# Two-layer retention, S5 and GLA encoder on one core: S5 parameters in two parts, S5 gates between the S5 output pairs, and another product order in the GLU

## The chip, the cores and the metric

The kernel runs on one core of a Trainium2 chip. The metric is the device time of one execution in microseconds; the kernel before has a median of 1593.84 us over three runs (1593.65 to 1594.63). The engines are TensorE (PE in the rows, with its weight loads as PEld), VectorE (DVE), ScalarE (ACT), GpSimd (POOL) and SyncE (SP), whose queue issues the DMAs.

## The reference

The input is 512 positions of 1024 features in float32, and there are two layers (`DEPTH = 2`). Each layer is

```
h = RMSNorm(x);  z = h @ w_in
A: retention, 4 heads, rotary q and k, fixed decay per head, head norm, swish gate
B: S5, 16 groups x 16 channels, complex diagonal state of 64, both directions, GELU, GLU projection
C: gated linear attention (GLA), 4 heads, gate from a low-rank projection, both directions, swish gate
merged = sum over the branches of sigmoid(h @ w_m + b) * (branch projection)
x += merged @ w_out
x += (relu(RMSNorm(x) @ w_up) ** 2) @ w_down
```

and a last RMSNorm follows. The GLU of branch B is `(y @ W1) * sigmoid(y @ W2)`. The S5 parameters of both layers (the discretised decays `exp(lambda * dt)`, their powers and the input factors) are worked out from 96 columns of a constant block: an exponential of `log_dt`, an exponential of `Re(lambda) * dt`, and a sine and cosine of `Im(lambda) * dt`, each as a polynomial on tiles of 128 x 32.

## The kernel before

Features lie on the partitions and the 512 positions on the free axis. The weights come as 128 chunks of 128 x 1024 a layer. `weights()` (L95) handles one: a DMA on SP's queue brings `raw` (three buffers, 512 KB), ScalarE casts it to `whi` (L108), and VectorE subtracts to make the remainder `wlo` (L109); five buffers hold such pairs. Activations are split the same way (`split()`, L112: `mh`, `ml`). `col_tile()` (L116) then issues three matmuls of 512 columns for each k: high times high, high times low, low times high. With 1024 inputs that is 24 matmuls for a column tile.

One layer runs in this order: the projections for S5 (`u`), GLA and retention; GLA; retention; the swish gates (`silu()`, L354); the sigmoid gates of the merge (`gate()`, L361, with numbers 16 to 23 for branch C, 0 to 7 for A and 8 to 15 for B), each group followed by its branch's projection; the GLU outputs of branch B in four pairs (`for j2`, L396); `w_out` (L412); then the feed-forward part.

What sets the order of instructions on each engine is the tile framework's scheduler, which goes by the order in which the code is written, by priorities (`hp(...)`) and by anchors (`issue_after`, which keeps an instruction behind another one). S5's own work is a generator, `self.bg`. `bg_steps(n, ...)` (L1023) pulls `n` of its pieces, anchored behind the evictions of the column tile just issued, so that they lie among the projections; in layer 0 the pieces also prepare the S5 matrices (60 pieces), in layer 1 that was done during layer 0's feed-forward part (24 pieces). `for _ in self.bg` (L393) pulls whatever is left.

`s5_params()` runs once, on GpSimd, with two casts and shifts and one reciprocal on VectorE. Its tiles are called `sp`; VectorE's part of an exponential is L818 (CAST) and L820 (shift). In the retention, a tile `za` of q or k gets its rotary form from three steps: GpSimd multiplies the swapped copy `rsw` (brought by DMA) by the sine (L634), VectorE multiplies `za` by the cosine (L635) and adds the two (L636); `qfb` (L666) is a decayed copy of q, also on GpSimd, also behind a DMA.

One GLU output goes through ScalarE (sigmoid of the second product, L404), GpSimd (times the gate, L405), VectorE (times the first product `ps1`, L406, and plus the sum of the other branches, L407), ScalarE (`mh`, L113) and VectorE (`ml`, L114).

Of the kernel before, what the change touches and what calls it, by code (L numbers as in the profile page):

```python
# [17 lines left out]
P = 128  # L18
# [21 lines left out]
class Hybrid:  # L40
# [147 lines left out]
    def run(self):  # L188
        nc, io = self.nc, self.io
        self.cst = self.one([P, 2432], "cst")  # L190
        xp = [self.sb.tile([P, 2, 512], F32, tag="xp", bufs=4, name=self.nm("xp")) for _ in range(KT // 2)]
        self.x = [xp[j // 2][:, j % 2, :] for j in range(KT)]
        self.chunk = 0
        self.pre = {}
        with self.hp(25000):
            nc.sync.dma_start(self.cst[:, C_SM:C_N], io["cst"][:, C_SM:])
            nc.sync.dma_start(self.x[0], io["xT"][:, 0, :])
            self.prefetch(0, 0, 2)
            nc.sync.dma_start(self.x[1], io["xT"][:, 1, :])
            nc.sync.dma_start(xp[1], io["xT"][:, 2:4, :])  # L200
            self.prefetch(0, 1, 2)
            for j in (2, 3):
                nc.sync.dma_start(xp[j], io["xT"][:, 2 * j:2 * j + 2, :])
            nc.sync.dma_start(self.cst[:, 0:C_MB], io["cst"][:, 0:C_MB])
        nc.sync.dma_start(self.cst[:, C_MB:C_SM], io["cst"][:, C_MB:C_SM])
        self.xsrc = [io["xT"][:, j, :] for j in range(KT)]
        self.sm = self.cst[:, C_SM:C_N]
        self.ident = self.cst[:, C_ID:C_ID + P]
        self.ones = self.cst[:, C_ONE:C_ONE + P]

        zero, warm = self.slot(s="warm"), self.ms()
        with self.hp(40000):
            nc.vector.memset(zero, 0.0)
            for _ in range(3):
                nc.tensor.matmul(warm, zero[:, 0:P], zero, start=True, stop=True)
        self.warm = lambda: nc.tensor.matmul(warm, zero[:, 0:P], zero, start=True, stop=True)
        accs, h = [], []
        with self.hp(35000):
            for j in range(KT):
                h.append(self.scaled_split(self.x[j], self.sm[:, SM_G1 + j:SM_G1 + j + 1]))  # L220
        with self.hp(30000):
            for j in range(KT):
                self.acc_sq(accs, self.x[j], j, nc.vector)
        for l in range(self.depth):
            self.chunk = 0
            h, accs = self.layer(l, h, accs)
# [78 lines left out]
    def layer(self, l, h, acc):  # L305
        nc, io = self.nc, self.io
# [18 lines left out]
        cv = [self.v_tiles(l, h, r) for _ in range(2)]  # L325
        if l == 0:
            with self.tc.issue_after(gl[-1][1].ins), self.tc.issue_after(self.gq.ins):
                self.s5_params()
        gla_o = []
        with self.hp(8000):  # L330
            pend = []
# [21 lines left out]

        def silu():  # L354
            sw = self.silu_tile(l, h, R)
            self.bg_steps(2, self.ev, self.mmi, self.aev)
            return sw

        yc = [self.gla_out(l, hd, gla_o[hd], silu()) for hd in range(4)]
# [1 line left out]
        def gate(j):  # L361
            w = self.weights(l)
            ps = self.col_tile(w, h)
            with self.hp(15000):
                g = self.gslot()
                ev = nc.vector.tensor_mul(g, ps, R)  # L366
                act = nc.scalar.activation(g, g, AF.Sigmoid, bias=self.smc(l, SM_BM, j))  # L367
            self.bg_steps(n, ev, self.mmi, act)
            return g
# [3 lines left out]
        for j2 in range(4):  # L373
            w = self.weights(l)
            for i in range(2):
                j = 2 * j2 + i
# [6 lines left out]
        for j4 in range(2):  # L383
            w = self.weights(l)
            for i in range(4):
                j = 4 * j4 + i
# [2 lines left out]
                    nc.vector.tensor_mul(ga[j], ga[j], ps)  # L389
                    nc.gpsimd.tensor_add(m[j], m[j], ga[j])  # L390
        ms = []
        gb = [gate(8 + j) for j in range(8)]
        for _ in self.bg:  # L393
            pass
        yb = self.ysplit(yb)
        for j2 in range(4):  # L396
            w = self.weights(l)
            for i in range(2):
                j = 2 * j2 + i
                ps1 = self.col_tile(w, yb, base=i * 512)  # L400
                ps2 = self.col_tile(w, yb, base=i * 512 + 256)
                with self.hp(15000):
                    s = self.gslot(s="glu")
                    nc.scalar.activation(s, ps2, AF.Sigmoid)  # L404
                    nc.gpsimd.tensor_mul(s, s, gb[j])  # L405
                    nc.vector.tensor_mul(s, s, ps1)  # L406
                    nc.vector.tensor_add(s, s, m[j])  # L407
                    hi, lo = self.slot(F32R, s="mh"), self.slot(F32R, s="ml")
                    self.split(hi, lo, s)
                    ms.append((hi, lo))  # L410
# [345 lines left out]
    def s5_params(self):  # L756
        nc = self.nc
# [4 lines left out]
        def T(dt=F32, keep=None):  # L762
            if keep:
                self.kn += 1
                return self.spk[:, (self.kn - 1) * N:self.kn * N]
            if self.tn % 16 == 0:
                self.spt = self.slot(shape=(P, 16, N), s="sp")
            o = self.spt[:, self.tn % 16, :]
            self.tn += 1
            return o if dt == F32 else o.bitcast(dt)  # L770
# [11 lines left out]
        def ts(a, s1, op0, s2=None, op1=None):  # L782
            o = T()
            if s2 is None:
                e.tensor_scalar(o, a, s1, None, op0)
            else:
                e.tensor_scalar(o, a, s1, s2, op0, op1)
            return o

        def poly(f, cs):  # L790
            q = ts(f, cs[-1], ALU.mult)
            for c in cs[-2::-1]:
                e.tensor_scalar(q, q, c, None, ALU.add)  # L793
                e.tensor_tensor(q, q, f, ALU.mult)
            return q
# [8 lines left out]
        def stt(a, s, b, op0, op1):  # L804
            o = T()
            e.tensor_scalar(o, a, s, None, op0)
            e.tensor_tensor(o, o, b, op1)
            return o
# [32 lines left out]
        s = poly(f2, [-1.0 / 6, 1.0 / 120, -1.0 / 5040, 1.0 / 362880])  # L841
        s = stt(s, 1.0, ph, ALU.add, ALU.mult)
        cm = poly(f2, [-0.5, 1.0 / 24, -1.0 / 720, 1.0 / 40320, -1.0 / 3628800])
        for _ in range(2):
            s2 = stt(cm, 1.0, s, ALU.add, ALU.mult)
            cm = stt(s, -2.0, s, ALU.mult, ALU.mult)
            s = ts(s2, 2.0, ALU.mult)
        c = ts(cm, 1.0, ALU.add)
        nr = stt(E, 1.0, cm, ALU.mult, ALU.mult)
        nr = tt(nr, em, ALU.add)  # L850
        ni = mul(E, s)
# [263 lines left out]
def _layout(v, depth=2):  # L1115
# [11 lines left out]
    def blk(w, c0, n=P):  # L1127
        k = w.shape[0] // P
        return w[:, c0:c0 + n].reshape(k, P, n).transpose(1, 0, 2).reshape(P, k * n)
# [5 lines left out]
    for l in range(depth):  # L1135
        w, wm = A("w_in")[l], A("w_merge_gate")[l]
        ba, bb, bc = A("w_branch_a")[l], A("w_branch_b")[l], A("w_branch_c")[l]
        wo, f1, f2 = A("w_out")[l], A("w_ff1")[l], A("w_ff2")[l]
        ch = [blk(w, c) for c in (1024, 1152)]
# [8 lines left out]
        ch += [np.concatenate([blk(bc, P * (2 * i + j)) for j in range(2)], 1) for i in range(4)]  # L1148
        ch += [blk(wm, P * i) for i in range(8)]
        ch += [np.concatenate([blk(ba, P * (4 * i + j)) for j in range(4)], 1) for i in range(2)]  # L1150
        ch += [blk(wm, 1024 + P * i) for i in range(8)]
        for i in range(4):
            ch += [np.concatenate([blk(bb, P * (2 * i + j) + o) for j in range(2) for o in (0, D)], 1)]
        ch += [blk(wo, P * i) for i in range(8)]
        for q in range(4):
# [6 lines left out]
        gw, gb = A("gla_w_gate")[l], A("gla_b_gate")[l]  # L1162
# [25 lines left out]
    i = np.arange(P)  # L1188
# [38 lines left out]
```

## Time and profile before

| | |
|---|---|
| median of three runs | 1593.84 us |
| the profiled execution | 1593.98 us, of which the span of the instructions is 1592.2 us |
| TensorE busy | 1561.0 us (98%), 7862 matmuls |
| VectorE busy | 942.7 us (59%) |
| ScalarE busy | 583.9 us (37%) |
| GpSimd busy | 220.1 us (14%) |
| mean granted clock of TensorE | 0.992 |

TensorE's busy time also counts the stretches in which it runs at half clock and those in which matmuls start further apart than 0.225 us, so 98% busy does not mean that only 2% can be had. A better measure of a stretch is how many matmuls it issued against how many would have fitted at the steady distance. The profiled execution lies 0.14 us above the median, and 1.8 us of it are outside the span.

### The profile page before, as it was taken

Reading aid. Unit: us, or ns where it says so; the run is one execution under the profiler, and the core shown is the slowest. Engines: PE = TensorE matmul, PEld = TensorE weight load, DVE = VectorE, ACT = ScalarE, POOL = GpSimd, SP = SyncE. Lnnn points to the kernel's source line nnn. Section 1 sums busy time; section 2 is a strip of 40 time slices with the busy share of each in tenths; the row PEclk is TensorE's granted clock in tenths of the full one; section 3 lists DMA queues with packets and bytes.
Section 4 is the critical chain, followed back from the end, with each engine's and each line's share of the span. In section 5 each row is a group of like instructions: output and inputs, shape, how many; then the busy total and the mean of one; then the engine's idle time right before and its main releaser. Section 6 shows DMA issues by size and latency. Waiting matters only on the chain.

```text
span 1592.2 us, 20246 instructions
## 1 busy us (share of the span) xinstructions
PE 1561.0 (98%) x7862; PEld 1306.5 (82%) x7862; DVE 942.7 (59%) x1579; ACT 583.9 (37%) x909; POOL 220.1 (14%) x351
## 2 busy tenths in 40 slices
PE   9998999999899999999999999999999999999997
PEld 6878888888788888888889888888868888888897
DVE  6776899854655747434658859844356534343353
ACT  5432444343434343423435332432334423232242
POOL 0185211121220000000101211203022000000001
PEclk9999999999999999999999999999999999999999
DMA  6513224233332323232434322342233232323221
GB/s 211 167 42 111 76 83 125 80 123 109 113 99 68 116 69 122 81 105 93 154 116 142 106 80 67 89 139 92 98 106 126 93 99 90 103 93 106 93 67 54
DMA packets 60512, 163.35 MB, mean 103 GB/s; under 512 B 10556, under 2 KB 17212, under 8 KB 60416
## 3 DMA queue, kind: packets, MB, share of 16 engines
q1 hardware_dynamic: 60096, 161.01, 31.6%
q8 instruction: 62, 1.02, 0.3%
q0 software_dynamic: 320, 1.05, 0.3%
q14 instruction: 34, 0.28, 0.1%
HBM read 147.11 MB, written 6.52 MB: 96 GB/s over the span
## 4 chain that ended last, share of the span: by engine, by line
PE 84%; DVE 7%; POOL 4%; ACT 2%; issue 2%; DMA 1%; SPq 0%; DVEq 0%; POOLq 0%; ACTq 0%
PE mm L126 25%; PE mm L127 25%; PE mm L125 25%; POOL glu L405 1%; PE mm L286 1%; PE mm L284 1%; PE mm L282 1%; DVE wlo L109 1%; PE ms L1091 1%; DMA dup<-zc 1%; POOL sp L793 1%; DVE glu L406 1%; DVE glu L407 1%; PE ms L1051 1%; PE ms L707 0%
## 5 line engine op out<-in xcount | busy, mean ns | idle before, releaser
L127 PE MATMUL mm<-hh,wlo 128*128 128x512 f32 x1136 | 445.8, 393 | 0.8 <-DVE wlo L109 0.8
L125 PE MATMUL mm<-hh,whi 128*128 128x512 f32 x1136 | 446.0, 393 | 0.0
L126 PE MATMUL mm<-hl,whi 128*128 128x512 f32 x1136 | 445.7, 392 | 0.0
L108 ACT CAST whi<-raw 128x1024 fp32r<-128x1024 f32 (+1 forms) x258 | 265.9, 1040 | 266.3 <-PE mm L127 137.5
L109 DVE TENSOR_TENSOR wlo<-raw,whi 128x1024 fp32r<-128x1024 f32 (+1 forms) x258 | 334.2, 1297 | 34.2 <-PE mm L126 28.1
L127 PEld LDWEIGHTS mm<-hh,wlo 128*128 128x128 f32 x1136 | 213.9, 188 | 44.9 <-DVE wlo L109 1.2
L125 PEld LDWEIGHTS mm<-hh,whi 128*128 128x128 f32 x1136 | 213.9, 188 | 44.7 <-issue 1.0
L126 PEld LDWEIGHTS mm<-hl,whi 128*128 128x128 f32 x1136 | 213.7, 188 | 44.0 <-issue 0.7
L126 PE MATMUL mm<-fl,whi 128*128 128x512 f32 (+1 forms) x576 | 210.8, 366 | 0.0
L127 PE MATMUL mm<-fh,wlo 128*128 128x512 f32 (+1 forms) x576 | 210.3, 366 | 0.0
L125 PE MATMUL mm<-fh,whi 128*128 128x512 f32 (+1 forms) x576 | 209.6, 366 | 0.0
L125 PEld LDWEIGHTS mm<-fh,whi 128*128 128x128 f32 x576 | 108.6, 189 | 17.8
L126 PEld LDWEIGHTS mm<-fl,whi 128*128 128x128 f32 x576 | 108.6, 189 | 17.6
L127 PEld LDWEIGHTS mm<-fh,wlo 128*128 128x128 f32 x576 | 108.6, 189 | 17.6 <-DVE wlo L109 0.2
L178 POOL TENSOR_TENSOR acc<-acc,sq 128x512 f32<-128x512 f32 (+1 forms) x30 | 35.3, 1176 | 552.9 <-ACT sq L177 552.9
L463 DVE TENSOR_TENSOR x<-x,mm 128x512 f32<-128x512 f32 x56 | 38.4, 685 | 121.8 <-PE mm L127 121.8
L438 ACT ACTIVATE ht<-ht 128x512 f32<-128x512 f32 x64 | 40.5, 632 | 175.1 <-DVE ht L437 175.1
L437 DVE SCALAR_TENSOR_TENSOR ht<-mm,R 128x512 f32<-128x512 f32 x64 | 44.1, 689 | 94.6 <-PE mm L127 83.4
L367 ACT ACTIVATE g<-g,cst 128x512 f32<-128x512 f32 x48 | 34.8, 725 | 148.1 <-DVE g L366 148.1
L114 DVE TENSOR_TENSOR fl<-ht,fh 128x512 fp32r<-128x512 f32 x64 | 44.3, 692 | 70.4 <-ACT fh L113 70.2
L366 DVE TENSOR_TENSOR g<-mm,R 128x512 f32<-128x512 f32 x48 | 32.9, 685 | 86.1 <-PE mm L127 82.6
L125 PE MATMUL mm<-y,whi 128*128 128x512 f32 x160 | 62.6, 391 | 0.7 <-DVE glu L406 0.7
(267 smaller groups left out, 2068.4 us busy)
## 6 DMA issues: line engine op xcount, KB each, us to landing
raw<-wst SPq DMA_DIRECT2D x254, 512.0 KB, 3.7
dup<-zc SPq DMA_DIRECT2D x32, 128.0 KB, 3.3
rsw<-za SPq DMA_DIRECT2D x32, 64.0 KB, 2.0
qfb<-za SPq DMA_DIRECT2D x16, 128.0 KB, 2.7
x<-xT SPq DMA_DIRECT2D x8, 256.0 KB, 3.9
xs<-x SPq DMA_DIRECT2D x8, 256.0 KB, 2.8
x<-xs SPq DMA_DIRECT2D x8, 256.0 KB, 4.2
outT<-out SPq DMA_DIRECT2D x8, 256.0 KB, 2.7
```

What stands on the lines that cost most here:

```text
L108: nc.scalar.copy(hi[:, s], raw[:, s])
L109: nc.vector.tensor_sub(lo[:, s], raw[:, s], hi[:, s].bitcast(F32))
L114: self.nc.vector.tensor_sub(lo, src, hi.bitcast(F32))
L125: nc.tensor.matmul(ps, hi[:, o:o + P], a, start=first and k == 0, stop=False)
L126: nc.tensor.matmul(ps, hi[:, o:o + P], b, start=False, stop=False)
L127: self.mmi = nc.tensor.matmul(ps, lo[:, o:o + P], a, start=False, stop=last and k == n - 1)
L178: return (eng or (nc.vector if j == KT - 1 else nc.gpsimd)).tensor_add(accs[0], accs[0], t)
L366: ev = nc.vector.tensor_mul(g, ps, R)
L367: act = nc.scalar.activation(g, g, AF.Sigmoid, bias=self.smc(l, SM_BM, j))
L437: ev = nc.vector.scalar_tensor_tensor(t, ps, 0.0, R2, ALU.max, ALU.mult)
L438: act = nc.scalar.square(t, t)
L463: ev = nc.vector.tensor_add(self.x[j], self.x[j], ps)
```

## The change

There are four edits.

1. `s5_params()` is made a generator with one `yield`. Its first part, up to the sine and cosine, is issued before the loop over the layers, where the start's own work is; the second part stays behind the GLA gates with the same anchors as before.
2. `silu()` pulls three S5 pieces, not two.
3. The eight gates of branch B (`gb`) are no longer all issued ahead of the S5 outputs: two are issued, then the rest of S5 is drained, and two more precede each further pair of GLU outputs. The weight chunks are laid out in this order too.
4. In the GLU, VectorE multiplies the gate by `ps1` (not the sigmoid's result by `ps1`), which can run beside the sigmoid; GpSimd then multiplies the sigmoid's result by that product, and VectorE adds the other branches.

```diff
+        self.params = self.s5_params()
+        next(self.params)
         for l in range(self.depth):
...
             with self.tc.issue_after(gl[-1][1].ins), self.tc.issue_after(self.gq.ins):
-                self.s5_params()
+                next(self.params, None)
...
-            self.bg_steps(2, self.ev, self.mmi, self.aev)
+            self.bg_steps(3, self.ev, self.mmi, self.aev)
...
-        gb = [gate(8 + j) for j in range(8)]
+        gb = [gate(8 + j) for j in range(2)]
         for _ in self.bg:
             pass
         yb = self.ysplit(yb)
         for j2 in range(4):
+            if j2:
+                gb += [gate(8 + 2 * j2 + i) for i in range(2)]
             w = self.weights(l)
...
                     nc.scalar.activation(s, ps2, AF.Sigmoid)
+                    nc.vector.tensor_mul(gb[j], gb[j], ps1)
                     nc.gpsimd.tensor_mul(s, s, gb[j])
-                    nc.vector.tensor_mul(s, s, ps1)
                     nc.vector.tensor_add(s, s, m[j])
...
         c = ts(cm, 1.0, ALU.add)
+        yield
         nr = stt(E, 1.0, cm, ALU.mult, ALU.mult)
...
-        ch += [blk(wm, 1024 + P * i) for i in range(8)]
         for i in range(4):
+            ch += [blk(wm, 1024 + P * (2 * i + j)) for j in range(2)]
             ch += [np.concatenate([blk(bb, P * (2 * i + j) + o) for j in range(2) for o in (0, D)], 1)]
```

The changed file has up to five lines more, so L634 of before is L638 after, L666 is L670, L818 and L820 are L822 and L824, L366 is L368, L404 is L408, and the GLU's three products and sums (L405, L406, L407) are L410, L409 and L411.

**GpSimd in layer 0's retention.** These are consecutive instructions of GpSimd before, around the second sine product of the retention (`rsw_1269`); `sp`, `pwt` and `cst` belong to the S5 parameters.

```order
L776 TENSOR_TENSOR cst<-sp_884 128x32
L887 TENSOR_TENSOR pwt_909<-cst 128x32
L888 TENSOR_TENSOR pwt_910<-cst 128x32
L634 TENSOR_TENSOR rsw_1269<-rsw_1269,sin_1192 128x512
L887 TENSOR_TENSOR pwt_909<-cst 128x32
L888 TENSOR_TENSOR pwt_910<-cst 128x32
```

And this is where the first sine products stand after.

```order
L895 TENSOR_TENSOR cst<-pwt_909,pwt_910 128x32x2
L894 TENSOR_TENSOR cst<-pwt_909,pwt_910 128x32x2
L638 TENSOR_TENSOR rsw_1228<-rsw_1228,sin_1192 128x512
L670 TENSOR_TENSOR qfb_1489<-qfb_1489,cst 128x512
L638 TENSOR_TENSOR rsw_1269<-rsw_1269,sin_1192 128x512
L670 TENSOR_TENSOR qfb_1496<-qfb_1496,cst 128x512
```

The parameters now end ahead of the first sine product, and the `qfb` product of the first `za` has come between the first and the second sine product. The first part of the parameters stands at the very start of GpSimd's list.

**VectorE at the start.** These are VectorE's instructions before, from the gate matrix `wg` to the statistics `nv` of the first norm.

```order
L486 TENSOR_TENSOR wlrs_268<-wlr_266,wlrs_268 128x8x16
L509 SCALAR_TENSOR_TENSOR wg_290<-wgh_301,cst,wgr_297 98x512
L109 TENSOR_TENSOR wlo_307<-raw_304,whi_306 128x1024
L109 TENSOR_TENSOR wlo_346<-raw_343,whi_345 128x1024
L158 TENSOR_SCALAR nv_151<-ms_142 128x4
```

And after:

```order
L490 TENSOR_TENSOR wlrs_371<-wlr_369,wlrs_371 128x8x16
L513 SCALAR_TENSOR_TENSOR wg_393<-wgh_404,cst,wgr_400 98x512
L822 CAST sp_179<-sp_179 128x32
L824 TENSOR_SCALAR sp_179<-sp_179 128x32
L109 TENSOR_TENSOR wlo_410<-raw_407,whi_409 128x1024
L109 TENSOR_TENSOR wlo_449<-raw_446,whi_448 128x1024
```

The second exponential's cast and shift now stand ahead of two weight splits. The first exponential's pair stands in the same way ahead of the first weight split, and on SP the DMA of the constants has come ahead of that of the first `x`.

**VectorE in layer 0's GLU.** These are VectorE's instructions before, from the last gate of branch B to the second GLU output.

```order
L366 TENSOR_TENSOR g_3548<-mm_3523,R_174 128x512
L406 TENSOR_TENSOR glu_3579<-glu_3579,mm_3565 128x512
L109 TENSOR_TENSOR wlo_3666<-raw_3663,whi_3665 128x1024
L407 TENSOR_TENSOR glu_3579<-glu_3579,g_2097 128x512
L114 TENSOR_TENSOR ml_3585<-glu_3579,mh_3584 128x512
L406 TENSOR_TENSOR glu_3602<-glu_3602,mm_3588 128x512
L407 TENSOR_TENSOR glu_3602<-glu_3602,g_2150 128x512
L109 TENSOR_TENSOR wlo_3718<-raw_3715,whi_3717 128x1024
L114 TENSOR_TENSOR ml_3608<-glu_3602,mh_3607 128x512
```

And after, from the second gate to the next pair's first gate:

```order
L368 TENSOR_TENSOR g_3344<-mm_3319,R_277 128x512
L409 TENSOR_TENSOR g_3310<-g_3310,mm_3361 128x512
L409 TENSOR_TENSOR g_3344<-g_3344,mm_3384 128x512
L411 TENSOR_TENSOR glu_3375<-glu_3375,g_2146 128x512
L109 TENSOR_TENSOR wlo_3444<-raw_3441,whi_3443 128x1024
L114 TENSOR_TENSOR ml_3381<-glu_3375,mh_3380 128x512
L411 TENSOR_TENSOR glu_3398<-glu_3398,g_2202 128x512
L109 TENSOR_TENSOR wlo_3478<-raw_3475,whi_3477 128x1024
L368 TENSOR_TENSOR g_3438<-mm_3413,R_277 128x512
L114 TENSOR_TENSOR ml_3404<-glu_3398,mh_3403 128x512
```

Both products with TensorE's output now stand ahead of the first sum, and gates of the next pair follow inside the pair. On TensorE the 24 matmuls of a pair of GLU outputs and 48 matmuls of two gates alternate, where the four pairs used to stand in one row.

## Rows read from the trace of the kernel before

**Rows 1.** The page's slices: busy tenths of VectorE in 40 equal slices.
```profile
DVE  6776899854655747434658859844356534343353
```

**Rows 2.** Table by stretch: PE, PEld, DVE, ACT, POOL busy (count), PE clock, DMA, GB/s.
```profile
330.00:375.00 45.00, 45.00 (x200) 37.26 (x199) 18.93 (x21) 16.93 (x19) 5.64 (x5) 1.00 0.46 151
375.00:425.00 50.00, 45.51 (x189) 35.87 (x188) 29.20 (x39) 20.80 (x31) 13.68 (x10) 0.97 0.33 111
1150.00:1200.00 50.00, 46.42 (x189) 35.59 (x188) 28.06 (x37) 19.23 (x30) 13.14 (x9) 0.97 0.33 113
```

**Rows 3.** Timeline of GpSimd, GLU: start, duration, instruction, idle before and releaser.
```profile
402.86 1.30 POOL L405 TENSOR_TENSOR glu<-glu,g 128x512 f32<-128x512 f32 x1 [2.68 <-ACT glu L404]
...
411.73 1.30 POOL L405 TENSOR_TENSOR glu<-glu,g 128x512 f32<-128x512 f32 x1 [2.67 <-ACT glu L404]
```

**Rows 4.** Timelines of ScalarE and VectorE, the last GLU output of layer 0.
```profile
411.06 0.59 ACT L404 ACTIVATE glu<-mm 128x512 f32<-128x512 f32 x1
...
415.17 0.69 DVE L114 TENSOR_TENSOR ml<-glu,mh 128x512 fp32r<-128x512 f32 x1 [0.69 <-ACT mh L113]
```

**Rows 5.** Timeline of TensorE, GLA and retention of layer 0: the two long waits.
```profile
103.44 0.72 PE L584 MATMUL ms<-v,sT 128*128 128x128 f32 x2 [2.44 <-DVE sT L562]
...
128.68 1.09 PE L658 MATMUL ms<-cst,za 128*128 128x128 f32 x4 [4.24 <-DVE za L636]
```

**Rows 6.** Table by stretch, the two stretches at half clock.
```profile
103.40:106.90 3.50, 3.46 (x9) 2.83 (x10) 3.31 (x7) 0.00 (x0) 2.94 (x9) 0.52 0.00 0
127.40:134.20 6.80, 5.52 (x31) 5.00 (x32) 6.53 (x6) 2.50 (x5) 6.56 (x16) 0.50 0.37 108
```

**Rows 7.** Table by stretch, GLA and retention of layer 0 and of layer 1.
```profile
50.30:147.20 96.90, 88.16 (x601) 79.03 (x600) 69.49 (x136) 38.20 (x91) 59.78 (x165) 0.95 0.35 104
843.80:926.00 82.20, 82.20 (x599) 75.05 (x598) 68.55 (x130) 39.90 (x92) 17.18 (x26) 1.00 0.39 114
```

**Rows 8.** Timeline of GpSimd, S5 parameters and sine products of layer 0.
```profile
83.97 1.02 POOL L787 TENSOR_SCALAR sp<-cst 128x32 f32<-128x32 f32 x1
...
90.12 0.29 POOL L793 TENSOR_SCALAR sp<-sp 128x32 f32<-128x32 f32 x1
...
91.17 1.15 POOL L793 TENSOR_SCALAR sp<-sp 128x32 f32<-128x32 f32 x1
...
126.38 1.25 POOL L634 TENSOR_TENSOR rsw<-rsw,sin 128x512 f32<-128x512 f32 x1
```

**Rows 9.** Timeline of VectorE in the same stretch.
```profile
87.67 0.21 DVE L818 CAST sp<-sp 128x32 int32<-128x32 f32 x1 [1.66 <-POOL sp L785]
...
90.89 1.28 DVE L109 TENSOR_TENSOR wlo<-raw,whi 128x1024 fp32r<-128x1024 f32 x1
...
100.71 0.20 DVE L818 CAST sp<-sp 128x32 int32<-128x32 f32 x1 [4.24 <-POOL sp L785]
...
127.67 0.87 DVE L636 TENSOR_TENSOR za<-za,rsw 128x512 f32<-128x512 f32 x1 [3.90 <-POOL rsw L634]
```

**Rows 10.** Timeline of VectorE and TensorE at the start.
```profile
5.88 0.68 DVE L109 TENSOR_TENSOR wlo<-raw,whi 128x512 fp32r<-128x512 f32 x1
...
6.61 0.50 PE L733 MATMUL mm<-hh,wlo 128*128 128x512 f32 x1
...
19.83 2.36 DVE L109 TENSOR_TENSOR wlo<-raw,whi 128x1024 fp32r<-128x1024 f32 x2 [0.20 <-ACT whi L108]
...
27.14 0.39 PE L127 MATMUL mm<-hh,wlo 128*128 128x512 f32 x1
```

**Rows 11.** Timeline of VectorE and TensorE, S5 pieces beside weight splits, both layers.
```profile
302.64 0.68 DVE L1077 TENSOR_TENSOR s5S<-s5a,s5b 128x508 f32<-128x508 f32 x1
303.24 1.21 DVE L109 TENSOR_TENSOR wlo<-raw,whi 128x1024 fp32r<-128x1024 f32 x1
...
307.55 0.39 PE L127 MATMUL mm<-hh,wlo 128*128 128x512 f32 x1
...
1018.46 0.50 PE L127 MATMUL mm<-hh,wlo 128*128 128x512 f32 x1 [0.79 <-DVE wlo L109]
```

## The prediction

> **What bounds the kernel now.** I read the slices first, then the table of stretches, then TensorE's waits and the timelines around them. TensorE is at work nearly all the time, so what an edit is worth is what it takes away from TensorE's late starts. In a stretch that waits for nothing, 200 matmuls take 45.00 us, 0.225 us each [rows 2]. Against that distance three places lose time. The GLU outputs: 189 matmuls in 50.00 us are 50.00 - 42.5 = 7.5 us lost, the same in layer 1, 15.0 in all [rows 2]. GLA and retention of layer 0: 601 matmuls take 96.90 us where layer 1 takes 82.20 for 599 [rows 7]; the two extra ones are 0.5, so layer 0 pays some 14.2 us for what only it does there, the S5 parameters. And the start, which waits for its input. VectorE is 80 to 90% busy in slices 5 to 9 [rows 1], which speaks for little room where S5 work comes on top. The profiled execution is 1593.98 us, 0.14 above the median of 1593.84; I count from 1593.98 and let the 0.14 stand.
>
> **GLU (edits 3 and 4).** Before, the chain of an output goes sigmoid, GpSimd product, two VectorE operations, cast, split. Every second output starts its GpSimd product 8.87 us after the last but one (411.73 - 402.86) [rows 3], while the 24 matmuls of a pair need 24 x 0.225 = 5.4 us. TensorE waits for the difference, and 0.5 us of each wait more, because the clock drops there (0.97 over both stretches [rows 2]). After, 48 gate matmuls (10.8 us) stand between two pairs: 16.2 us a pair against a chain of 8.87 or less. The first three pairs are thus covered. The last is followed by w_out, whose first column tile reads output 8 as the last of eight k, so 21 matmuls or 4.7 us behind the last product. The chain from sigmoid to the end of the split took 415.86 - 411.06 = 4.8 us [rows 4]; one VectorE product of 0.7 now runs beside the sigmoid, which leaves 4.1; to it come 0.3 until the sigmoid starts and some 1.0 because the pair's first output is still in the chain (8.87 / 2 - 0.7 = 3.7 us an output, TensorE makes one in 2.7). 5.4 against 4.7: 0.5 to 0.7 us of wait a layer, and I take 0.5. Without the gain of edit 4 it would be 2.1. So -15.0 + 1.0 = **-14.0**, between -10.8 and -15.0.
>
> **Retention and GLA (edit 1, second part).** TensorE waits 2.44 us for GLA's masked scores, which stand on VectorE behind a cast that waited 4.24 us for GpSimd's parameters, and 4.24 us for the second rotary sum, whose sine product stood on GpSimd behind parameters until 126.38 [rows 5, 8, 9]. After each wait TensorE ran at 1.2 GHz, half its other level, for 3.5 and 6.8 us [rows 6]. The 9 matmuls of the first cost 3.46 - 9 x 0.225 = 1.4 to 1.8 us more than usual; the 31 of the second are mostly short ones, and I take 1.2 of the 0 to 2.8 (half of 5.52) that they can have lost. 2.44 + 4.24 + 1.8 + 1.2 = 9.7. The casts now run in the start, and one reciprocal is left in GLA. What comes late next: by the order the first `qfb` product stands ahead of the second sine product, behind a DMA of the first rotary tile. Counted from the rows (first sine product near 111 instead of 115.98 by the same order, sum, DMA, `qfb`, second sine product at 1.25, sum at 0.87) the second sum ends at 119 to 121; TensorE gets there at 128.68 - 4.24 = 124.4, less the 4.2 us gained ahead of it, near 120. I take 0.5 left: **-9.2**. The bounds are -5 (the second wait halved only) and -14.2 (the layers alike).
>
> **The start (edit 1, first part).** TensorE's list gets nothing; VectorE gets two casts and shifts that wait for GpSimd. The first stands ahead of the first weight split, 5.88, whose reader starts at 6.61, so no slack [rows 10]. In the trace this cast comes 3.7 us after the parameters' first operation (87.67 - 83.97) [rows 8, 9]. If the constants land at 3.9 us (my estimate, between 3 and 5, since weights from the same queue were already being split at 5.88), the split starts at 7.6: 1.7 us late, partly made good because TensorE waits for input there anyway; with 0.3 for the `x` DMA that now comes second, I take 2.0. The second cast comes 16.7 us after the first operation (100.71 - 83.97), with a memset of 1 us near 21.6. Behind it stands the split of the first z chunk, 1.2 us, read at 27.14 [rows 10]: it may come as late as 25.5. That holds if GpSimd is as quick as it was there. It may not be: a parameter operation of 0.29 us took 1.15 when VectorE split a weight chunk beside it (90.89 to 92.17) [rows 8, 9], and at the start VectorE is busy without a gap for some 11 us. If GpSimd got nothing done in those, the cast would come at 33 to 35, and TensorE would stop for up to 9.6. So **+2.0**, between 0 and +11.6.
>
> The Trainium skill, page "SBUF — State Buffer", section "Who interferes with whom", states a rule that speaks against this place: a VectorE instruction with two SBUF inputs and a GpSimd instruction that reads SBUF hold the same read interface in turn, for the whole instruction, and whichever issues first blocks the other. The 1.15 us row agrees. By that rule GpSimd gets one short operation in after each of some 16 VectorE operations; the cast would come near 26.5, and the start would cost 3 us, not 2.
>
> **S5 pieces earlier (edits 2 and 3).** Nothing is added, but VectorE's S5 instructions move ahead of weight splits. By the order, thirteen more of them (0.68 each, two longer scans; some 9.4 us) stand ahead of the split that started at 303.24, whose first reader began at 307.55 [rows 11]. That split had 3.1 us to spare, so it may be 6.3 us late at most; VectorE's idle time there and the S5 matmuls that move up on TensorE take up most of it. In layer 1 the tightest split has five more (3.4 us) ahead, and a split there already kept TensorE waiting 0.79 [rows 11]. I take 2 + 1 = **+3.0**, between 0 and +9.7. The last S5 output is not late by edit 3: between its last matmul and its first reader 153 others stand (34 us).
>
> **Sum.** -14.0 - 9.2 + 2.0 + 3.0 = -18.2, so 1593.98 - 18.2 = **1575.8 us**.
>
> **The rivals.**
> - *Only the GLU pays.* GLA and retention find another late step (the `qfb` product ahead of the sine product, or a weight split late on a full VectorE), and give 0 to 2 of the 9.2. For it: VectorE's slices there are full. Against it: layer 1 does the same work with TensorE busy throughout [rows 7]. -14.0 - 1 + 5 = 1584.
> - *GpSimd is shut out at the start.* The parameters end 9.6 us late: 1575.8 + 9.6 = 1585.4. For it: the 1.15 us row. Against it: nearly all parameter operations in [rows 8]'s stretch took under 0.4 us on a VectorE that was also mostly busy.
> - *Everything comes off.* Layer 0 equals layer 1 (-14.2), nothing at the start or from S5, nothing left in the GLU: 1593.98 - 15.0 - 14.2 = 1564.8. Against it: the tight splits in [rows 11].
> - *The GLU does not do what it says:* ScalarE and GpSimd still hand each output on in turn and the gates only shift the wait, so that half of the loss stays: 1575.8 + 7 = 1583.
> - *Slower: VectorE is the bound.* The place is its queue ahead of weight splits: at the start (11.6), and in layer 0 fifteen (11.7 us) and in layer 1 twelve S5 instructions (8.9 us) ahead of one split at worst, all uncovered: 32.2 against 14.0 + 9.2 = 23.2, so 1603. It decides from where 72% of the 32.2 reaches TensorE. Against it: splits had 3 us and more to spare at most places.
>
> **How the numbers follow.** The forecast gets 0.54, only the GLU 0.14, GpSimd shut out 0.10, everything 0.10, the GLU at half 0.06; slower 0.04, and 0.02 for a mixture that ends near no change. A difference under 0.2% (3.2 us) can hardly be told from none in this kernel; within it lies only the last. So faster 0.93, same 0.03, slower 0.04. The range takes the forecast with its bounds and the three cases around 1584, and most of the case at 1564.8: 1565 to 1586.
>
> **What would show it.** In the profile after, the stretch of the GLU pairs and gates has TensorE at 0.225 us a matmul and full clock in both layers, with one wait under 1 us at w_out. In layer 0 the waits for the masked scores and for the rotary sum are gone or under 1 us, and the stretch from 50.30 takes 84 to 89 us. At the start GpSimd's parameters end before 27, and VectorE's two casts show waits for GpSimd. New waits of TensorE for `wlo` add up to 3 us in the S5 stretches. The prediction is wrong if such waits exceed 8 us, if the first z tile starts after 30 us, or if GLU waits stay in the places where they were.

## The result and the profile after

The changed kernel takes 1572.35 us (median of four runs, 1571.93 to 1572.37), the kernel before 1594.0: the ratio is 0.9863, with a 95% interval of 0.9846 to 0.9880. The forecast was 1575.8 in a range of 1565 to 1586. The profiled execution of the changed kernel took 1572.37 us, with a span of 1570.6.

First the head of the page after: span, busy time and share, number of instructions.

```profile
span 1570.6 us, 20256 instructions
...
PE 1551.2 (99%) x7862; PEld 1303.0 (83%) x7862; DVE 946.8 (60%) x1579; ACT 585.0 (37%) x909; POOL 228.2 (15%) x351
```

The work is the same; GpSimd is 8 us longer busy (228.2 against 220.1). Now the table by stretch of the kernel after: the GLU in both layers, then GLA and retention of layer 0 and of layer 1, in the columns of [rows 2].

```profile
366.00:411.00 45.00, 45.00 (x200) 37.26 (x199) 25.17 (x29) 18.04 (x25) 8.65 (x6) 1.00 0.38 127
1126.00:1171.00 45.00, 45.00 (x200) 37.28 (x199) 22.86 (x29) 17.91 (x25) 8.77 (x6) 1.00 0.41 141
...
51.50:137.10 85.60, 83.14 (x600) 75.26 (x599) 70.23 (x132) 39.80 (x93) 28.88 (x69) 1.00 0.39 118
828.30:910.60 82.30, 82.30 (x599) 75.10 (x598) 68.58 (x130) 40.02 (x92) 17.27 (x26) 1.00 0.37 111
```

With gates and GLU pairs taking turns, 200 matmuls fit in 45.00 us in either layer, the steady distance; before it was 189 in 50 us [rows 2]. GLA and retention of layer 0 went from 96.90 us [rows 7] to 85.60, at full clock, and those of layer 1 stayed where they were. And TensorE's waits: line, releaser, us in total, times, longest.

```profile
PE ms L164 <- DVE dg L162: 2.9, 1, 2.9
PE mm L735 <- ACT whi L108: 2.0, 1, 2.0
PE ms L215 <- DVE warm L213: 1.5, 1, 1.5
PE ms L662 <- DVE za L640: 1.1, 1, 1.1
PE mm L125 <- DVE u L749: 1.0, 1, 1.0
PE mm L125 <- ACT whi L108: 0.8, 1, 0.8
PE mm L127 <- DVE wlo L109: 0.8, 2, 0.6
```

The rotary sum keeps TensorE waiting 1.1 us (4.24 before [rows 5]), the wait of 2.44 us for GLA's masked scores is gone, and no GLU wait is left. New are 2.0 us at the very start and 1.0 us at the start of layer 1.

Stage by stage, from the first matmul of one stage to that of the next:

| stage | before | after | difference |
|---|---|---|---|
| start, to the first value projection of GLA | 50.3 | 51.5 | +1.2 |
| GLA and retention, to the first retention state, layer 0 | 96.9 | 85.6 | -11.3 |
| rest of retention, swish gates, S5, gates, GLU, w_out, to the first down projection, layer 0 | 347.6 | 341.0 | -6.6 |
| MLP of layer 0 from there, and start of layer 1 | 349.0 | 350.3 | +1.3 |
| as the second row, layer 1 | 82.3 | 82.3 | 0 |
| as the third row, layer 1 | 345.3 | 338.9 | -6.4 |
| rest | 320.8 | 321.1 | +0.3 |

That makes -21.5, the difference of the spans but for rounding. In the third and the sixth row the GLU's loss of 7.5 us is gone, and 0.9 and 1.1 us have come in. Two matmuls (0.45 us) that stood in the second row before stand in the third now, so half of the 0.9 is a shift of the border, and the second row's -11.3 holds the same 0.45.

### The profile page after: what moved, and what is told of

It reads as the page before. It is cut to its first block, busy times and chain, and to the rows that moved or that the text cites. A ratio compares the mean times of both kernels' runs of the same rounds, so it can differ in the third digit from the quotient of the medians.

```text
span 1570.6 us, 20256 instructions
## 1 busy us (share of the span) xinstructions
PE 1551.2 (99%) x7862; PEld 1303.0 (83%) x7862; DVE 946.8 (60%) x1579; ACT 585.0 (37%) x909; POOL 228.2 (15%) x351
## 4 chain that ended last, share of the span: by engine, by line
PE 89%; DVE 5%; issue 2%; ACT 1%; DMA 1%; POOL 1%; SPq 0%; DVEq 0%; POOLq 0%; ACTq 0%
PE mm L125 26%; PE mm L127 26%; PE mm L126 26%; PE mm L286 1%; PE mm L288 1%; PE mm L284 1%; PE ms L1096 1%; DVE wlo L109 1%; PE ms L1056 1%; DMA dup<-zc 0%; PE ms L711 0%; PE ms L712 0%; PE ms L697 0%; PE ms L563 0%; PE ms L684 0%
## 5 line engine op out<-in xcount | busy, mean ns | idle before, releaser
L109 DVE TENSOR_TENSOR wlo<-raw,whi 128x1024 fp32r<-128x1024 f32 (+1 forms) x258 | 340.6, 1322 | 37.1 <-PE mm L126 29.1
L441 DVE SCALAR_TENSOR_TENSOR ht<-mm,R 128x512 f32<-128x512 f32 x64 | 44.2, 690 | 93.6 <-PE mm L127 82.3
L368 DVE TENSOR_TENSOR g<-mm,R 128x512 f32<-128x512 f32 x48 | 32.9, 686 | 72.0 <-PE mm L127 68.5
```

Of the source, the lines that this page charges most:

```text
L109: nc.vector.tensor_sub(lo[:, s], raw[:, s], hi[:, s].bitcast(F32))
L441: ev = nc.vector.scalar_tensor_tensor(t, ps, 0.0, R2, ALU.max, ALU.mult)
```

## The experiments

**Each edit alone, and the two GLU edits together.** The theory was that of the prediction: losses are private to their stages, and add.

Edit 1 alone (`s5_params` in two parts):

```diff
+        self.params = self.s5_params()
+        next(self.params)
...
-                self.s5_params()
+                next(self.params, None)
...
         c = ts(cm, 1.0, ALU.add)
+        yield
```

> The kernel before with edit 1 alone (parameters in two parts). Theory, the losses are private to their stages and add: GLA and retention of layer 0 lose the 11.2 us that the changed kernel lost there, the start costs 1.2 us, the GLU stretches stay: 1594.0 - 11.2 + 1.2 = 1584 (1582 to 1586). Rival, the retention's gain needs the S5 pieces to be moved too, since VectorE is full there: 1589 or more. TensorE's first matmul with weights should start near 7.9 us instead of 5.74 in both.

It took 1569.4 us (ratio 0.9844, 0.9829 to 0.9858): 15 us below the forecast, and no slower than all four edits together. GLA and retention of layer 0 took 83.4 us where 85.7 was expected, so 2.3 of the 15 are there; most of the surplus is in the third and the sixth row of the table of stages, which took 6.8 and 4.7 us less than before. The table by stretch shows where: the 45 us of the GLU in both layers, in the kernel with edit 1 alone.

```profile
355.00:400.00 45.00, 44.42 (x196) 36.31 (x195) 32.43 (x37) 19.58 (x30) 12.48 (x8) 1.00 0.36 122
1135.00:1180.00 45.00, 44.41 (x195) 36.33 (x195) 37.16 (x39) 21.16 (x31) 14.92 (x10) 1.00 0.35 116
```

196 and 195 matmuls in 45 us, where the kernel before issues 167 and 166 in such a stretch. The GLU's loss is gone, though no line of the GLU has changed. This did away with the theory that edits 3 and 4 were needed for it, and left my reason for the loss in doubt.

Edit 4 alone (the product order):

```diff
                     nc.scalar.activation(s, ps2, AF.Sigmoid)
+                    nc.vector.tensor_mul(gb[j], gb[j], ps1)
                     nc.gpsimd.tensor_mul(s, s, gb[j])
-                    nc.vector.tensor_mul(s, s, ps1)
```

> The kernel before with edit 4 alone (product order). Theory, the chain of a pair gets shorter by the VectorE product that now runs beside the sigmoid (two times 0.7), 8.87 to 7.4 us, but stays longer than the 5.4 us of TensorE's matmuls: of the 7.5 us lost in each layer about half comes back, 1594.0 - 7 = 1587 (1584 to 1590). Rival A, the order alone is what pays: 1580. Rival B, the GpSimd product now waits for VectorE behind a weight split, and nothing comes back: 1593 to 1595.

1587.45 us (0.9957, 0.9942 to 0.9972): as the theory had it, nearly half of the loss comes back, 181 matmuls in 45 us in both layers. The pace was not the 7.4 us expected: the eight sigmoids of layer 0 run from 378.95 to 408.01, which is 8.3 us a pair.

Edit 3 alone (gates between the pairs):

```diff
-        gb = [gate(8 + j) for j in range(8)]
+        gb = [gate(8 + j) for j in range(2)]
...
+            if j2:
+                gb += [gate(8 + 2 * j2 + i) for i in range(2)]
...
-        ch += [blk(wm, 1024 + P * i) for i in range(8)]
         for i in range(4):
+            ch += [blk(wm, 1024 + P * (2 * i + j)) for j in range(2)]
```

> The kernel before with edit 3 alone (gates between the pairs), old product order. Theory, a chain of 8.87 us lies under 16.2 us of matmuls for the first three pairs, and what is left is the tail of the last pair, some 2 us a layer: 1594.0 - 15.0 + 4 = 1583 (1581 to 1585). Rival, the product order is what pays: 1590 or more.

1578.8 us (0.9904, 0.9889 to 0.9919), 4 us better than expected: no tail of the last pair is left, TensorE has no wait in the GLU of either layer.

Edits 3 and 4, the two diffs above:

> The kernel before with edits 3 and 4. Theory, the whole loss of the two GLU stretches goes: 1594.0 - 15 = 1579 (1578 to 1581). Rival, the S5 drain after only two gates makes TensorE wait for the last S5 output without edit 2: up to 5 us a layer less gain, 1584 or more.

1579.15 us (0.9906, 0.9889 to 0.9922). The theory's value, but edit 4 adds nothing to edit 3, and the S5 drain needs no edit 2.

**Why edit 1 alone frees the GLU.** The order of ScalarE's instructions differs there. In the kernel before, its queue holds sigmoid, cast (`mh`), sigmoid, cast; with edit 1 alone it holds sigmoid, sigmoid, cast, sigmoid, cast. In the first order the sigmoid of an output stands behind the cast of the output before, and that cast waits for GpSimd and two VectorE operations. These are rows of the kernel before, of ScalarE, then one of VectorE and one of TensorE:

```profile
393.33 0.59 ACT L404 ACTIVATE glu<-mm 128x512 f32<-128x512 f32 x1
396.78 0.62 ACT L113 CAST mh<-glu 128x512 fp32r<-128x512 f32 x1 [2.86 <-DVE glu L407]
397.31 1.05 ACT L108 CAST whi<-raw 128x1024 fp32r<-128x1024 f32 x1
398.26 0.59 ACT L404 ACTIVATE glu<-mm 128x512 f32<-128x512 f32 x1
...
404.19 0.69 DVE L406 TENSOR_TENSOR glu<-glu,mm 128x512 f32<-128x512 f32 x1 [1.18 <-POOL glu L405]
...
396.08 0.50 PE L125 MATMUL mm<-y,whi 128*128 128x512 f32 x1 [0.39 <-DVE glu L406]
```

From 376.48 us on TensorE issued 84 matmuls with `y`, seven outputs of 12, before its first wait at 396.08. The last of the fifth output's matmuls started at 389.86, but its sigmoid starts at 398.26, after ScalarE has stood idle 2.86 us in front of a cast. So each output begins when the one before is all but done, whatever TensorE has ready. I call this theory Q, and its rival C (the prediction's reason): the chain of an output is too long for the 5.4 us of a pair's matmuls. Theory Q is tested by moving the cast and split of an output behind the next sigmoid:

```diff
-        ms = []
+        ms, todo = [], []
...
-                    nc.scalar.activation(s, ps2, AF.Sigmoid)
+                    sg = nc.scalar.activation(s, ps2, AF.Sigmoid)
+                    if todo:
+                        with self.tc.issue_after(sg.ins):
+                            self.split(*todo.pop(0))
...
-                    self.split(hi, lo, s)
+                    todo.append((hi, lo, s))
...
+        with self.hp(15000):
+            self.split(*todo.pop(0))
```

> The kernel before with one edit: the sigmoid of a GLU output is issued ahead of the cast and split of the output before it, so that ScalarE's queue holds sigmoid, sigmoid, cast, sigmoid, cast and not sigmoid, cast, sigmoid, cast. Product order and gates are as before. Theory Q, the 7.5 us a layer are lost because each sigmoid stands on ScalarE behind a cast that waits for the whole chain of the output before it: the loss falls to some 1 us a layer, 1594.0 - 13 = 1581 (1579 to 1583). Rival C, the chain is too long for 5.4 us of matmuls whatever the queue's order, and only other matmuls or a shorter chain help: 1590 or more.

1581.9 us (0.9920, 0.9905 to 0.9935). In the whole program only instructions of the GLU and a few matmuls of w_out stand in another order than before; products and sums are the same. The split has an operation on VectorE too (`ml`), so eight of VectorE's places in each layer change with ScalarE's; but VectorE's order was not what held the loop before, since VectorE stood idle there 1.18 to 1.77 us in front of each product from the second on and waited for GpSimd, and GpSimd waited for the sigmoid [rows 3]. The two stretches, and ScalarE's timeline in the first:

```profile
372.00:417.00 45.00, 44.42 (x194) 35.82 (x193) 32.93 (x38) 20.54 (x30) 12.80 (x9) 1.00 0.36 118
1148.00:1193.00 45.00, 44.68 (x195) 35.94 (x194) 34.75 (x39) 21.16 (x31) 15.54 (x10) 1.00 0.36 116
```

```profile
391.17 0.59 ACT L404 ACTIVATE glu<-mm 128x512 f32<-128x512 f32 x1
392.63 0.62 ACT L113 CAST mh<-glu 128x512 fp32r<-128x512 f32 x1 [0.87 <-DVE glu L410]
393.17 0.59 ACT L404 ACTIVATE glu<-mm 128x512 f32<-128x512 f32 x1
396.05 0.62 ACT L113 CAST mh<-glu 128x512 fp32r<-128x512 f32 x1 [2.29 <-DVE glu L410]
396.57 1.05 ACT L108 CAST whi<-raw 128x1024 fp32r<-128x1024 f32 x1
397.52 0.59 ACT L404 ACTIVATE glu<-mm 128x512 f32<-128x512 f32 x1
```

Some 13 us come back with one call moved, and this pair takes 6.35 us (397.52 - 391.17), not 8.87 [rows 3]. A cast here belongs to the output before the one whose sigmoid has just run, so the chain of one output runs beside that of the next. Rival C falls as far as it says that the order cannot help. A part of it stays: over all eight sigmoids of layer 0 (380.96 to 404.62) a pair takes 6.8 us (9.0 before, 379.40 to 411.06), still more than 5.4. The eighth sigmoid thus comes 23.66 - 7 x 2.7 = 4.8 us later than the matmuls alone would have it, and w_out reads output 8 only 4.7 us behind the last product, so one wait of 0.45 us is left in that layer. Before, the same sum gives 12.8 us.

Edit 2 alone (three S5 pieces in a swish gate, a change of one figure) was the next test, since its ScalarE order had also come out with the sigmoids ahead. What makes the scheduler choose one order or the other is not shown by any run.

```diff
-            self.bg_steps(2, self.ev, self.mmi, self.aev)
+            self.bg_steps(3, self.ev, self.mmi, self.aev)
```

> The kernel before with edit 2 alone (three S5 pieces in a swish gate). By ScalarE's order, the GLU's sigmoids stand here one output ahead of the casts in both layers, as in the kernel with edit 1 alone and unlike before, though the GLU's code is that of before. Theory Q: the GLU stretches lose some 1 us a layer, the retention stays as it was, S5 costs 0 to 3: 1594.0 - 13 + 1 = 1582 (1580 to 1585). Rival, the GLU gain of the kernel with edit 1 alone came from edit 1 itself: 1593 to 1597.

1580.71 us (0.9910, 0.9895 to 0.9925); 194 and 196 matmuls in 45 us. That the total fits is in part luck. GLA and retention of layer 0 also fell from 96.9 to 91.9 us, which I had not expected: the wait for the rotary sum is there (3.9 us), the 2.44 us for the masked scores are not. The third and the sixth row of the table of stages together fell by 9.7, not by 12, so the S5 pieces cost about the 3 us that the expectation put at the end of its range. Which instruction's move frees GLA stays open.

And the reverse: edit 1 with the DMA of the first `x` put first. It turns ScalarE's order back to sigmoid, cast, sigmoid, cast.

```diff
-            nc.sync.dma_start(self.x[0], io["xT"][:, 0, :])
+            with self.hp(60000):
+                nc.sync.dma_start(self.x[0], io["xT"][:, 0, :])
```

> Edit 1 alone, with the DMA of the first x ahead of that of the constants, as before. By ScalarE's order the GLU's sigmoids and casts alternate here again, as in the kernel before. Theory Q: the 7.5 us a layer come back, and the start gains up to 1: 1569.4 + 13 - 0.5 = 1582 (1580 to 1584). Rival, edit 1 frees the GLU in some other way: 1568 to 1570.

1584.42 us (0.9937, 0.9922 to 0.9952), 15 us above edit 1 alone and 0.4 above the range. ScalarE's timeline and the two stretches:

```profile
379.88 0.59 ACT L407 ACTIVATE glu<-mm 128x512 f32<-128x512 f32 x1
383.39 0.62 ACT L113 CAST mh<-glu 128x512 fp32r<-128x512 f32 x1 [2.91 <-DVE glu L410]
383.91 0.59 ACT L407 ACTIVATE glu<-mm 128x512 f32<-128x512 f32 x1
387.36 0.62 ACT L113 CAST mh<-glu 128x512 fp32r<-128x512 f32 x1 [2.85 <-DVE glu L410]
387.89 1.04 ACT L108 CAST whi<-raw 128x1024 fp32r<-128x1024 f32 x1
388.84 0.58 ACT L407 ACTIVATE glu<-mm 128x512 f32<-128x512 f32 x1
```

```profile
368.00:413.00 45.00, 40.46 (x167) 31.57 (x166) 26.71 (x36) 18.81 (x28) 12.64 (x9) 0.96 0.30 99
1142.00:1187.00 45.00, 41.49 (x166) 31.48 (x165) 25.46 (x34) 17.69 (x27) 10.30 (x8) 0.96 0.29 95
```

Each sigmoid begins where a cast ends, after 2.85 to 2.91 us in which ScalarE has nothing it may do; a pair takes 8.96 us again (388.84 - 379.88), and the 7.5 us a layer are back: the third and the sixth row of the table of stages are 348.1 and 345.2 us, 12.0 more than with edit 1 alone. The other 3.0 are in GLA and retention (86.4 against 83.4), where this kernel's instructions stand in another order too. A DMA moved by one place at 0 us turned the scheduler's order of instructions at 380 and 1150 us.

With that DMA first and the sigmoids held ahead by hand (edit 1, this diff and that of the sigmoids):

> Edit 1, the first x ahead of the constants, and the sigmoid of a GLU output issued ahead of the cast of the one before it. Theory Q: 13 below the kernel without the last of the three, 1568 to 1570, 3 below the changed kernel although edits 2, 3 and 4 are not in it. Rival C: as without the last, 1580 or more.

1569.93 us (0.9844, 0.9827 to 0.9860), as theory Q has it: the two rows with the GLU take 12.4 us less than without the last diff. GLA and retention take 2.6 less and the start 1.8 more, which theory Q does not speak of.

**What edits 2, 3 and 4 are worth beside edit 1.** The changed kernel without edit 2:

```diff
-            self.bg_steps(3, self.ev, self.mmi, self.aev)
+            self.bg_steps(2, self.ev, self.mmi, self.aev)
```

> The changed kernel without edit 2 (two S5 pieces in a swish gate, as before). Theory, edit 2 frees nothing: even at two pieces layer 0's 60 pieces are all pulled before the gates of branch B (12 + 24 + 8 + 24 places), so the last S5 output is in time, and VectorE has less to do ahead of the tight splits: 1570 to 1573. Rival, without edit 2 the last S5 output or the drain is late by 3 to 5 us: 1576 or more.

1570.39 us (0.9849, 0.9834 to 0.9863). Edits 1 and 4, put together from the two diffs above:

> Edits 1 and 4. By ScalarE's order the sigmoids stand one output ahead of the casts here. Theory Q, the queue's order decides and the product order adds little: as with edit 1 alone, 1569.4 (1568 to 1571). Rival, the two gains add as in the prediction: 1594 - 11 - 7 + 1 = 1577.

1570.68 us (0.9853, 0.9838 to 0.9868). Edit 4 does shorten the pace further, to 6.1 us a pair (sigmoids of layer 0 from 370.48 to 391.74) against 6.7 with edit 1 alone (365.96 to 389.52), but TensorE had no wait for this chain left that it could save. Edits 1 and 3, likewise:

> Edits 1 and 3. Sigmoids and casts alternate on ScalarE here, but 48 gate matmuls lie between the pairs. Theory, cover by the gates and the queue's order are two cures of the same 15 us, and edits 2 and 4 add nothing to either: 1570 to 1573, as the changed kernel. Rival, edit 4 is needed for the tail of the last pair: 1574 to 1576.

1570.17 us (0.9848, 0.9834 to 0.9863). All three as the theory had it, and all a little under the changed kernel. By stages, the kernel without edit 2 takes 349.0 us from the MLP of layer 0 to layer 1's GLA (350.3 with it), and 1.2 us less in layer 1's S5 stretch, 0.6 in layer 0's; it loses 1.0 in the retention. So edit 2 costs about 2 us by the stages. The comparison by intervals doesn't separate these kernels (each has its ratio inside the others' intervals); the runs of the changed kernel (1571.93 to 1572.37) do lie above those without edit 2 (1569.91 to 1570.59), though beside these the kernel before took 1594.4 and not 1594.0.

**Why in two parts.** The changed kernel with both parts of the parameters at the start:

```diff
-        self.params = self.s5_params()
-        next(self.params)
+        self.s5_params()
...
-            with self.tc.issue_after(gl[-1][1].ins), self.tc.issue_after(self.gq.ins):
-                next(self.params, None)
+            pass
...
-        yield
```

> The changed kernel with both parts of the parameters at the start. In the changed kernel GpSimd ended the first part at 42.7 us, was idle until 52.30, and took 10.6 us for the second part; by the order the reciprocal's input comes early. Theory, the second part fits in, the gates' products come 1 to 2 us later than 52.30 but are first read at 73.66, and retention has nothing of it left: 1571 to 1573. Rival, the gates' products behind it make GLA late, or the reciprocal holds VectorE ahead of a weight split: 1575 or more.

1580.26 us (0.9910, 0.9894 to 0.9927): 8 us slower, and GLA with retention of layer 0 takes 93.7 us, against 85.6. The rival was right that GLA gets late, but not in its reason. Timelines of GpSimd, VectorE and TensorE:

```profile
51.55 0.47 POOL L778 TENSOR_TENSOR cst<-sp,sp 128x32 f32<-128x32 f32 x2
...
52.05 1.22 DVE L531 TENSOR_TENSOR_SCAN cum<-scm,a 64x512 f32<-64x512 f32 x1 [8.17 <-POOL cst L778]
...
56.70 0.58 PE L283 MATMUL mm<-whi,hh 128*128 128x256 f32 x1 [5.61 <-DVE zc L267]
```

The cumulative sum of the first GLA gate waited 8.17 us for the operation that ends GpSimd's parameters; behind it on VectorE stood the eviction of a projection, and TensorE waited 5.61 us for its PSUM. The scan reads no parameter, so the row names a releaser that made none of its operands; what the wait is for (a shared buffer would be one guess) is not shown.

## Why the prediction was right, and where not

The sign, the size and the two main places were right. Against the -18.2 forecast, -21.65 was measured. That four edits bring this is right as a sum, but edit 1 alone brings as much: the losses are not private to their stages, because each edit also changes the scheduler's order elsewhere.

**GLU: -14.0 forecast, -15.0 measured.** The size was right, and so was the cover by the gates; the reason for the loss was not. The step "the chain takes 8.87 us, the matmuls of a pair 5.4, TensorE waits for the difference" reads a period as if it were a length that can't be overlapped. It was the period of a loop that ScalarE's queue closed: sigmoid behind cast. The kernel with the sigmoids ahead, which has the same chain, fell to 6.8 us a pair, and TensorE's loss with it from 15 to some 2.5 us in both layers together. Nor did TensorE wait for the difference at each pair: in layer 0 it ran seven outputs ahead and then had four waits, of 4.5 us in all. The gates between the pairs help because they give the closed loop 16.2 us; they are one of two cures, and edit 1 happened to bring the other with it. In the changed kernel the casts still stand ahead of the next sigmoids, so there it is the gates that hide them. That no tail was left (0.5 a layer in the sum) follows from edit 3 alone as well.

**GLA and retention: -9.2 forecast, -11.3 measured** (the other kernels with edit 1's two parts took 83.4 to 86.9 us for this stretch, so it is good to some 2 us). The step is right: what stood behind the parameters on GpSimd came free, both waits and both half-clock stretches went. The sine product that came at 126.38 [rows 8] now stands here (GpSimd's timeline, then TensorE's):

```profile
113.69 1.32 POOL L670 TENSOR_TENSOR qfb<-qfb,cst 128x512 f32<-128x512 f32 x1 [3.77 <-DMA qfb<-za]
116.58 2.06 POOL L638 TENSOR_TENSOR rsw<-rsw,sin 128x512 f32<-128x512 f32 x1 [1.57 <-DMA rsw<-za]
```

```profile
121.03 0.63 PE L662 MATMUL ms<-cst,za 128*128 128x128 f32 x4 [1.10 <-DVE za L640]
```

It waits for its own DMA, not for the `qfb` product ahead of it, and TensorE comes 1.1 us too early (0.5 was taken). The waits were sized right: TensorE's idle time in this stretch fell from 96.90 - 88.16 = 8.74 to 85.60 - 83.14 = 2.46, by 6.3 us, where 2.44 + 4.24 - 0.5 = 6.2 was forecast. What was too small is the clock's term: TensorE's busy time, which counts half clock and wider spacing too, fell by 5.0 us (0.45 of it the shifted border), where 1.8 + 1.2 = 3.0 was taken.

**Start: +2.0 forecast, +1.2 measured, and that not by the step forecast.** Timelines after, of ScalarE, VectorE, TensorE, GpSimd and VectorE again:

```profile
4.83 1.28 ACT L184 ACT_TABLE_LOAD   x1 [4.83 <-DMA xp<-xT]
6.12 0.72 ACT L184 ACTIVATE hh<-xp,cst 128x512 fp32r<-128x512 f32 x1
...
7.54 0.23 DVE L822 CAST sp<-sp 128x32 int32<-128x32 f32 x1
7.81 0.18 DVE L824 TENSOR_SCALAR sp<-sp 128x32 int32<-128x32 int32 x1
7.90 1.36 DVE L109 TENSOR_TENSOR wlo<-raw,whi 128x512 fp32r<-128x512 f32 x2
...
7.92 0.59 PE L735 MATMUL mm<-hh,whi 128*128 128x512 f32 x1 [1.99 <-ACT whi L108]
...
10.88 0.61 POOL L797 TENSOR_SCALAR sp<-sp 128x32 f32<-128x32 f32 x1
11.57 0.55 POOL L798 TENSOR_TENSOR sp<-sp 128x32 f32<-128x32 f32 x1
12.20 0.61 POOL L797 TENSOR_SCALAR sp<-sp 128x32 f32<-128x32 f32 x1
...
23.49 0.21 DVE L822 CAST sp<-sp 128x32 int32<-128x32 f32 x1 [2.63 <-POOL sp L789]
```

The first split starts at 7.90 (7.6 forecast), but the cast ahead of it did not wait for GpSimd, whose first operation began at 3.21 (3.9 was taken for the constants). What came late is ScalarE: the first `x` landed behind the constants, at 4.83 us (3.93 before; 0.3 was taken for this), and the activation table, loaded at 0.74 us in the kernel before, is now loaded behind that DMA. Even so the +1.2 is not a fixed price of edit 1. Four other kernels with the same start (edit 1 alone, with edit 3, with edit 4, and with both parts at the start) begin GLA at 50.7 to 50.9, among the kernels that leave the start alone (50.3 to 51.1). The profiled executions that began it later are this one (51.5), that without edit 2 (51.6) and the one with `x` first and the sigmoids ahead (52.6), and only in these was the granted clock under full speed in the first 20 us. Here it is after, then with edit 1 alone: stretch, TensorE's busy time (count), clock, DMA share, GB/s.

```profile
0.00:10.00 10.00, 6.55 (x10) 0.91 0.74 228
10.00:20.00 10.00, 10.00 (x39) 0.92 1.04 369
...
0.00:10.00 10.00, 7.84 (x13) 1.00 0.78 232
10.00:20.00 10.00, 9.72 (x40) 1.00 1.03 363
```

Ahead of the lower clock TensorE had waited 1.99 us at 7.92; with edit 1 alone it waited 0.69 us there. Three of the eight kernels with edit 1 have such a start and none of the six without it; with one profile each, that does not show whether edit 1 makes it likelier. The second cast came at 23.49, between the prediction's two values (21.6, and 26.5 by the rule), ahead of the 25.5 from which it would have cost anything. GpSimd was not shut out, though its first part ended at 42.7 us, long after the 27 of the prediction's list of signs; it then stood idle until 52.30, so this cost nothing.

The Trainium skill, page "SBUF — State Buffer", section "Who interferes with whom", has a GpSimd instruction that reads SBUF and a VectorE instruction with two SBUF inputs contend for one read interface. The rows agree: with VectorE busy back to back, GpSimd's short operations from 10.21 to 12.89 us begin 0.63 to 0.69 us apart, one for each VectorE operation of 0.7, instead of 0.37.

**S5: +3.0 forecast, at most +2 measured** (0.9 and 1.1 beside the GLU, with 0.45 of the 0.9 a shift of the border), with waits for `wlo` of 0.8 in all, both in layer 1. Layer 1's part is edit 2's, as the kernel without it showed; in layer 0 TensorE has no wait in this row, and where the rest of the 0.9 lies stays open.

**Not forecast: +1.3 at the start of layer 1,** where no edit touches the code:

```profile
810.93 0.47 PE L125 MATMUL mm<-hh,whi 128*128 128x512 f32 x1 [0.99 <-DVE u L749]
```

The order of TensorE's matmuls is the same there as before, but this one waits for VectorE's eviction of `u`, which suggests that its PSUM buffer is another one. Without edit 2 the wait isn't there, and with edit 2 alone it isn't either (349.0 us for the row, as before); why stays open.

The rivals: GLU alone (1584), GpSimd shut out (1585) and the GLU at half (1583) did not come about, the slower case was far off. Of the case "everything comes off" (1564.8) the GLU gave all of its 15.0, the retention 11.3 of 14.2. One argument for "only the GLU" was misread: VectorE's slices of GLA and retention in layer 0 are the second to the fourth, and they show 7, 7 and 6 [rows 1]; 8, 9, 9 and 8 are the fifth to the eighth, where the S5 pieces lie, and the ninth is 5.

## What to carry to other kernels

When a short chain over several engines repeats and its period is longer than its supplier's, look at the order in each in-order queue before calling the chain too long: if an instruction that starts the next round stands behind one that ends this round, the rounds run one after the other. Here moving the end of a round behind the start of the next in the code brought back 13 of 15 us, and it held against a scheduler that may otherwise choose either order. Whether the chain itself is short enough is a second question: at 6.8 us a pair against 5.4 it was not, and only w_out's matmuls behind it hid that. And where a scheduler sets the order, test each edit alone and compare stages: here nearly half of one edit's gain came from a place that it does not touch, and another edit cost some 2 us.

## What was not expected of the hardware

A GpSimd operation on 128 x 32 elements took 0.25 to 0.29 us alone and mostly 0.49 to 0.61 beside a busy VectorE. The chain of 41 of them up to the second cast took 20.3 us (3.21 to 23.49, with one memset of 0.95 us in between) where it had taken 16.7 among GLA's work (83.97 to 100.71, with six short memsets): a fifth more and not twice as much.
